# Whole fp32 probability products for four of ten key tiles in two layers' attentions, and a new table of planned durations

## The chip, the cores and the metric

One Trainium2 chip; the kernel runs on one of its cores. The metric is the device time of one execution in microseconds (us). Three executions of the kernel before took 4149.66, 4151.16 and 4156.11 us; their median, 4151.16 us, is the time before.

## The reference, cut to what matters

Everything is float32. The program is two blocks, one after the other. The first block has two layers. Each layer has, over 1024 tokens and 256 context tokens, two kinds of attention with six heads each ("MLA": keys of 96 numbers a head; "GQA": keys of 64 numbers, two key heads for six query heads), a depthwise convolution with 31 taps, gates and an output projection. The attention is plain softmax attention over 1280 keys for the tokens, and (in the first layer only) over the 256 context keys for the context:

```python
s = jnp.einsum('bqgrd,bkgd->bgrqk', qi, k).astype(jnp.float32) * scale
p = jax.nn.softmax(s, axis=-1).astype(v.dtype)
return jnp.einsum('bgrqk,bkgv->bqgrv', p, v)
```

The second block (a gated linear attention, an index selection of the 256 best keys, a sparse attention, a feed-forward net and norms) isn't touched by the change in its arithmetic.

## The kernel before, in words

**Precision.** The program gives TensorE its operands as `float32r` or as `float32`. Where they are `float32r`, a number is split first into a high and a low half, each a `float32r` tile: `N.split` makes the high half with a copy that rounds (line 293 on VectorE or line 284 on ScalarE) and the low half with a subtraction (line 325 on VectorE or line 327 on GpSimd). A product of two split operands is three matmuls: high by high, high by low, low by high.

**The attention.** `attend` (in `layer`, in `block1`) writes one unit of work: one head and one chunk of 512 queries (chunks 0 and 1), or of the 256 context queries (chunk 2, first layer only). A unit first finds the row maximum of the scores (line 368's reductions, and transposes), and then loops over key tiles of 128 keys: ten for chunks 0 and 1, two (tiles 8 and 9) for chunk 2. In each key tile it multiplies keys and queries into PSUM (three passes in MLA, two in GQA), takes the exponential on ScalarE into a float32 page `p` of 128 keys by 512 queries, splits `p` into `ph` and `pl`, and adds three products of 512 columns to the accumulator: `vh` by `ph`, `vl` by `ph`, `vh` by `pl`. A column of ones beside the values gives the sum of the probabilities at once. There are 24 units of 512 queries in each layer, and 12 of 256 in the first.

**The values.** `vtiles` makes the value tiles, two key tiles to a page pair (`a` for the high halves, `b` for the low ones), five page pairs a call, by two transposes, two copies and two subtractions for each, and fills in the ones and zeros on GpSimd. A layer calls it five times (three pairs of MLA heads, two GQA key heads).

**What sets the order.** The program lists its operations in the order of the mathematics, with some merged into others by `merge` and `pipeline`: a unit's start is laid beside the loop of the unit before it. Then a planner, `Plan.schedule`, simulates the five engines with a duration for each operation (the functions `c_act`, `c_v`, `c_p`, and those in `copy`, `ts`, `scale`, `mm`, `tr`), and writes each engine's instructions down in the order in which they started in that simulation. Where an operation may go to either of two engines (a copy to ScalarE or VectorE, a subtraction to VectorE or GpSimd), the simulation also picks the engine: the cheaper one, unless its queue makes the other one sooner. On the chip each engine runs its list in order and waits for what isn't ready. The planner works on the whole program at once, and its buffers (89 pages, 8 PSUM banks) are given out in that same simulation.

**Names.** `pg` is a page in SBUF (128 partitions by 512 numbers), `ps` a PSUM bank, `sm` a small tile, `c` a constant. Line 384 issues every matmul, 388 every transpose, 284 every ScalarE operation, 335 VectorE's operations with a scalar (the convolution's taps and `modulation2` among them).

Of the kernel before, what the change touches and what calls it, by code (L numbers as in the profile page):

```python
# [4 lines left out]
F32 = mybir.dt.float32  # L5
F32R = mybir.dt.float32r
# [18 lines left out]
def _mt(w):  # L25
    k, m = w.shape
    return w.reshape(k // 128, 128, m // 128, 128).transpose(2, 1, 0, 3).reshape(m // 128, 128, k)


V1 = dict(norm=0, bmod=8, qn=32, kvn=34, gq=35, gk=36, dwb=37, lnw=39, lnb=41, pwb=43, dw=45)  # L30
NV1 = 45 + 62
# [130 lines left out]


class Op:
    __slots__ = ("alts", "reads", "writes", "emit", "idx", "succ", "npred", "allocs", "table", "bufs", "tag", "pr", "late")


BASIC = ("Copy", "Identity", "Square", "Abs", "Relu")
# [4 lines left out]
class Plan:  # L173
# [37 lines left out]
    def op(self, alts, reads, writes, emit, table=None):  # L211
        o = Op()
        o.alts = alts
        o.reads = [x for x in reads if isinstance(x, View)]
        o.writes = [x for x in writes if isinstance(x, View)]
        o.emit = emit
        o.table = table
        o.tag = self.tag
        o.late = self.late
        self.cur.append(o)  # L220
        return o
# [37 lines left out]
        return out  # L259

    def c_act(self, n, src, extra=0):
        return (n * 0.833 + (52 if isinstance(src, View) and src.psum else 93) + extra) / 1000

    def act(self, out, in_, func, bias=None, scale=1.0, accum=None, alts=None):
        nc = self.nc
# [31 lines left out]
    def copy(self, out, in_, engs="av"):  # L297
        a = {}
        n = out.n
        if "v" in engs:  # L300
            a["v"] = (n * (1.04 if in_.psum else 0.52) + 68) / 1000
        if "a" in engs:
            return self.act(out, in_, "Copy", alts=a)
        return self.op(a, [in_], [out], lambda e: self._copy(e, out, in_))
# [2 lines left out]
        return {"v": self.nc.vector, "p": self.nc.gpsimd}[e]  # L307

    def c_v(self, n, ex=0):
        return (n * 1.04 + 68 + ex) / 1000  # L310

    def c_p(self, n):
        return (n * 2.1 + 150) / 1000

    def tt(self, out, in0, in1, op, engs="v"):
        o = getattr(OP, op)
# [23 lines left out]
    def ts(self, out, in0, s1, s2, op0, op1=None, accum=None):  # L340
        o0 = getattr(OP, op0)
        k = {} if op1 is None else {"op1": getattr(OP, op1)}

        def emit(e):
            if accum is not None:
                k["accum_out"] = real(accum)
            self.nc.vector.tensor_scalar(out=real(out), in0=real(in0), scalar1=real(s1), scalar2=real(s2), op0=o0, **k)  # L347

        return self.op({"v": (out.n * (1.04 if in0.psum or accum is not None else 0.52) + 130 + (127 if accum is not None else 0)) / 1000},
                       [in0, s1, s2], [out, accum], emit)  # L350

    def scale(self, out, in_, col):

        n = out.n

        def emit(e):
            if e == "a":
                self.nc.scalar.activation(real(out), real(in_), AF.Copy, scale=real(col))
            else:
                self.nc.vector.tensor_scalar(out=real(out), in0=real(in_), scalar1=real(col), scalar2=None, op0=OP.mult)  # L360

        return self.op({"v": (n * (1.04 if in_.psum else 0.52) + 130) / 1000, "a": self.c_act(n, in_, 93)},
                       [in_, col], [out], emit)

    def red(self, out, in_, op="max"):
# [13 lines left out]

    def mm(self, out, lhsT, rhs, start, stop, cost=None):  # L380
        n = rhs.n
        c = cost or max(n * 1.676 if rhs.ap.dtype == F32 or n < 256 else n * 0.4219, 60) / 1000
        return self.op({"t": c}, [lhsT, rhs] + ([] if start else [out]), [out],
                       lambda e: self.nc.tensor.matmul(real(out), lhsT=real(lhsT), rhs=real(rhs), start=start, stop=stop))  # L384

    def tr(self, out, in_, ident):
        return self.op({"t": 0.109}, [in_, ident], [out],
                       lambda e: self.nc.tensor.transpose(real(out), real(in_), real(ident)))  # L388

    def dma(self, out, in_, cost=None):  # L390
# [10 lines left out]
    def schedule(self, window=1500, dwindow=1200, boost=0, queue=0.25, verbose=False):  # L401
# [8 lines left out]
        for o in ops:  # L410
            preds = set()
            bufs = {}
# [110 lines left out]
        while len(order) < N:  # L523
            progress = False
            for e in engs:
                while busy[e] <= now + 1e-9:

                    h = ready[e]
                    skipped = []
                    got = None  # L530
                    best_alt = None
                    while h:
                        i, o = heapq.heappop(h)
                        if issued[o.idx]:
                            continue
                        ok = admissible(o, e)
                        if ok and len(o.alts) > 1:

                            m = min(o.alts, key=lambda x: o.alts[x])
                            if m != e:  # L540
                                wait = max(0.0, busy[m] - now) + queue * min(len(ready[m]), 12)
                                if wait + o.alts[m] < o.alts[e]:
                                    ok = False
                        if ok and e == "a" and o.table is not None and o.table != table:
                            if best_alt is None:
                                best_alt = o
                            skipped.append((i, o))
                            if len(skipped) > 24:
                                break
                            continue  # L550
                        if ok:
                            if best_alt is not None and i > best_alt.pr + 60:
                                skipped.append((i, o))
                                break
                            got = o
                            break
                        skipped.append((i, o))
                        if len(skipped) > 200:
                            break
                    if got is None and best_alt is not None:  # L560
                        got = best_alt
                        skipped = [s for s in skipped if s[1] is not got]
                    for s in skipped:
                        heapq.heappush(h, s)
                    if got is None:
                        break
                    o = got
                    issued[o.idx] = True
                    progress = True
                    c = o.alts[e]  # L570
                    pre = None
                    if e == "a" and o.table is not None and o.table != table:
                        pre = o.table
                        table = o.table
                        c += 1.3
                    new = [b for b in o.allocs if b.slot is None]
                    for b in new:
                        if b.cls in free:
                            need[b.cls][head:o.idx] += 1
                            first[b] = head  # L580
                        b.slot = free[b.cls].pop() if b.cls in free else 0
                    if e == "d":
                        st = max(now + 1.5, dmabw[0])
                        dmabw[0] = st + c
                        fin = st + c + 0.6
                        busy[e] = now + 0.45
                        stat[e] += c
                    else:
                        busy[e] = now + c
                        fin = now + c  # L590
                        stat[e] += c
                    order.append((now, e, o, pre, new))
                    seq += 1
                    heapq.heappush(ev, (fin, 0, seq, o, e))
                    heapq.heappush(ev, (busy[e], 1, seq, None, e))
                    while head < N and issued[head]:
                        head += 1
# [174 lines left out]
def block1(N, O, early, dbg=None):  # L772
# [85 lines left out]
    def layer(l, h, xsrc, xdst, after):  # L858
# [209 lines left out]
        def attend(c, passes, qmax, kmax, nrow, negrow, vt, pos, scale, gate, yf, units, main, back=1):  # L1068
# [27 lines left out]
            for kt in kts:  # L1096
# [3 lines left out]
                N.mm(s, [(kk[kc][:, ks], qq) for kk, qq in passes])  # L1100
                p = fpg(c)
                P.act(p, s, "Exp", scale=scale)
                ph, pl = pair(c)
                split(ph, pl, p)
                vh, vl = (x[:, pos * 64:pos * 64 + 128] for x in vt[kt])
# [21 lines left out]
        def vtiles(src, sel):  # L1127

            out = {}
            for i in range(5):  # L1130
                a, b = P.pg(F32R), P.pg(F32R)
                kc, j = (2, 0) if i == 4 else (i // 2, (i % 2) * 256)
                tp = P.ps(256)
                for t in range(2):
                    P.tr(tp[:, t * 128:(t + 1) * 128], src[kc][:, j + t * 128:j + (t + 1) * 128], N.ident)
                tv = tp.rearrange("p (t b e) -> p t b e", t=2, b=2)
                av = a.rearrange("p (t b e) -> p t b e", t=2, b=2)
                bv = b.rearrange("p (t b e) -> p t b e", t=2, b=2)
                for dst, s_ in sel:
                    P.copy(av[:, :, dst, 0:64], tv[:, :, s_, :])  # L1140
                    lo(bv[:, :, dst, 0:64], tv[:, :, s_, :], av[:, :, dst, 0:64])
                P.memset(av[:, :, 0, 64:128].f(), 1.0)
                P.memset(bv[:, :, 0, 64:128].f(), 0.0)
                for t in range(2):
                    out[2 * i + t] = (a[:, t * 256:t * 256 + 192], b[:, t * 256:t * 256 + 192])
# [895 lines left out]
```

## Time and profile before

| what | value |
|---|---|
| median of three runs | 4151.16 us |
| the profiled execution's own time | 4150.0 us |
| its span, first to last instruction | 4148.1 us |
| mean granted TensorE clock | 0.98 of full speed |
| TensorE matmul busy | 94% of the span |
| VectorE busy | 80% |
| ScalarE busy | 49% |
| GpSimd busy | 34% |

In the profile PE is TensorE's matmul, PEld its weight load, DVE VectorE, ACT ScalarE, POOL GpSimd. A matmul's record lasts from its start to the modelled end of its pipeline, so neighbouring records overlap: the busy time of PE is a union of such records, and the distance from one record to the next is what a matmul costs in a dense stream. Each row of a group ends with the group's busy time, the mean duration of one, and the idle time of the engine just before them with the instruction that ended it. In the profile's list of forms a float32r matmul and a float32 one look alike (`f32`).

### The profile page before, as it was taken

To read this page: it belongs to the slowest core of one execution; us is meant where nothing else is said; L and a number is where in the kernel's file an instruction comes from. 1 tells how busy PE (TensorE), PEld (TensorE's weight loads), DVE (VectorE), ACT (ScalarE), POOL (GpSimd) and SP (SyncE) were. 2 spreads that over 40 slices of the span, in tenths; PEclk is the share of its full clock that TensorE was granted. 3 is DMA by queue.
4 is the path that set the end of the run, shared out by engine and by line. 5 is a ranking of instruction groups with operands and counts; after the bars stand their busy time and mean duration, and the time that the engine had idled before them with its cause. 6 is when DMAs were issued, how large, how long until landed. Compare 5 with 4: busy or idle time off the path is not lost. (4 is left out here: it accounts for less than half of the span.)

```text
span 4148.1 us, 54250 instructions
## 1 busy us (share of the span) xinstructions
PE 3908.4 (94%) x18536; PEld 3153.5 (76%) x18536; DVE 3306.3 (80%) x5640; ACT 2036.4 (49%) x3969; POOL 1430.2 (34%) x1257
## 2 busy tenths in 40 slices
PE   7989998989989998999999999999999999999988
PEld 4768766667877776778878878888878788888867
DVE  8995899997896789985999996388886865455588
ACT  5244576774334566763545551366663432222245
POOL 4542455663142344552223441011132411121153
PEclk8999999999999999999999999999999999999998
DMA  7132211123323110042111142100044411111121
GB/s 254 62 117 72 62 54 53 50 70 114 110 83 99 39 34 26 16 133 94 67 44 54 67 142 77 62 31 30 32 144 152 137 51 49 49 41 46 56 82 57
DMA packets 184981, 311.88 MB, mean 75 GB/s; under 512 B 22912, under 2 KB 46208, under 8 KB 184704
## 3 DMA queue, kind: packets, MB, share of 16 engines
q1 hardware_dynamic: 184704, 308.42, 23.0%
q8 instruction: 146, 2.39, 0.2%
q14 instruction: 131, 1.07, 0.1%
HBM read 237.81 MB, written 62.39 MB: 72 GB/s over the span
## 5 line engine op out<-in xcount | busy, mean ns | idle before, releaser
L384 PE MATMUL ps<-pg,pg 128*128 128x512 f32 (+4 forms) x17200 | 3843.6, 380 | 119.1 <-ACT pg L284 43.5
L384 PEld LDWEIGHTS ps<-pg,pg 128*128 128x128 f32 (+2 forms) x17200 | 3009.0, 190 | 798.5 <-ACT pg L284 72.9
L327 POOL TENSOR_TENSOR pg<-pg,pg 128x512 fp32r<-128x512 f32 (+4 forms) x935 | 1355.7, 1462 | 2338.7 <-ACT pg L284 1301.7
L284 ACT ACTIVATE pg<-pg 128x512 fp32r<-128x512 f32 (+9 forms) x1529 | 875.5, 601 | 893.5 <-DVE pg L335 240.6
L325 DVE TENSOR_TENSOR pg<-pg,pg 128x512 fp32r<-128x512 f32 (+8 forms) x1126 | 956.2, 868 | 218.7 <-ACT pg L284 162.6
L284 ACT ACTIVATE pg<-ps 128x512 f32<-128x512 f32 (+9 forms) x1351 | 686.8, 557 | 801.4 <-PE ps L384 597.4
L325 DVE TENSOR_TENSOR pg<-ps,pg 128x128 fp32r<-128x128 f32 (+9 forms) x690 | 381.3, 567 | 209.2 <-PE ps L384 146.3
L335 DVE SCALAR_TENSOR_TENSOR pg<-ux,c,pg 128x512 f32<-128x512 f32 x416 | 348.7, 867 | 9.6 <-ACT pg L284 2.2
L368 DVE TENSOR_REDUCE sm<-ps 128x1 f32<-128x512 f32 (+1 forms) x492 | 326.1, 679 | 9.6 <-PE ps L384 7.0
L293 DVE CAST pg<-pg 128x512 fp32r<-128x512 f32 (+4 forms) x387 | 226.9, 596 | 72.0 <-ACT pg L284 34.0
L284 ACT ACTIVATE pg<-ps,c 128x512 f32<-128x512 f32 (+1 forms) x182 | 127.3, 708 | 250.0 <-PE ps L384 218.5
L335 DVE SCALAR_TENSOR_TENSOR pg<-pg,c,pg 128x512 f32<-128x512 f32 (+3 forms) x242 | 220.1, 946 | 5.5 <-ACT pg L284 5.2
L388 PE MATMUL ps<-c,pg 128*128 128x128 f32 (+1 forms) x796 | 180.2, 274 | 14.3 <-DVE pg L293 5.8
L293 DVE COPY ux<-ps 128x512 f32<-128x512 f32 x83 | 57.3, 690 | 143.3 <-ACT pg L284 133.6
L1523 DVE MAX8 sm<-ux 128x8 f32<-128x384 f32 (+5 forms) x192 | 168.8, 887 | 3.3
L1524 DVE MATCH_REPLACE8 ux<-sm,ux 128x384 f32<-128x384 f32 (+5 forms) x192 | 167.7, 875 | 0.0
L384 PE MATMUL ps<-pg,c 128*128 128x512 f32 (+3 forms) x196 | 85.2, 502 | 74.9 <-DVE pg L325 28.6
L388 PEld LDWEIGHTS ps<-c,pg 128*128 128x128 f32 (+1 forms) x796 | 107.6, 141 | 40.3 <-issue 6.2
L284 ACT ACTIVATE pg<-pg,sm 128x512 f32<-128x512 f32 (+2 forms) x192 | 116.2, 606 | 11.2 <-DVE sm L347 10.7
L384 PEld LDWEIGHTS ps<-pg,c 128*128 128x128 f32 (+2 forms) x196 | 33.6, 176 | 105.7 <-DVE pg L325 31.6
L671 ACT ACT_TABLE_LOAD x84 | 107.8, 1283 | 1.5
L1778 DVE CUSTOM_DVE_ANT_0 pg<-ps,pg 128x512 f32<-128x512 f32 (+3 forms) x176 | 100.0, 575 | 8.5 <-PE ps L384 6.3
(74 smaller groups left out, 1017.2 us busy)
## 6 DMA issues: line engine op xcount, KB each, us to landing
d<-pg SPq DMA_DIRECT2D x202, 256.0 KB, 2.1
pg<-d SPq DMA_DIRECT2D x178, 256.0 KB, 3.3
pg<-in_w2a SPq DMA_DIRECT2D x108, 256.0 KB, 2.8
pg<-in_wmod SPq DMA_DIRECT2D x96, 256.0 KB, 3.1
pg<-in_wup SPq DMA_DIRECT2D x88, 256.0 KB, 2.7
pg<-in_win SPq DMA_DIRECT2D x80, 256.0 KB, 3.3
pg<-in_wout SPq DMA_DIRECT2D x64, 256.0 KB, 3.3
pg<-in_wdn SPq DMA_DIRECT2D x48, 256.0 KB, 2.7
```

The source lines that it names most:

```text
L284: nc.scalar.activation(real(out), real(in_), fn, scale=real(scale), **k)
L293: self.nc.vector.tensor_copy(real(out), real(in_))
L325: self.nc.vector.tensor_tensor(out=real(out), in0=real(in0), in1=real(in1), op=o)
L327: self.nc.gpsimd.tensor_tensor(out=real(out), in0=real(in0), in1=real(in1), op=o)
L335: self.nc.vector.scalar_tensor_tensor(out=real(out), in0=real(in0), scalar=real(scalar), in1=real(in1), op0=o0, op1=o1)
L368: lambda e: self.nc.vector.tensor_reduce(out=real(out), in_=real(in_), axis=AX.X, op=o))
L384: lambda e: self.nc.tensor.matmul(real(out), lhsT=real(lhsT), rhs=real(rhs), start=start, stop=stop))
L388: lambda e: self.nc.tensor.transpose(real(out), real(in_), real(ident)))
L671: nc.scalar.preload_act_table_set(pre)
L1523: P.vec(P.c_v(n), [w], [m8], lambda e, m8=m8, w=w: nc.vector.max(real(m8), real(w)))
L1524: P.vec(P.c_v(n), [w, m8], [w], lambda e, m8=m8, w=w: nc.vector.match_replace(real(w), real(m8), real(w), MARK))
L1778: lambda e, p=p, s=s, n=n, m=mk[t, b], a=sm[:, b:b + 1]: nc.vector.tensor_tensor_reduce(out=real(p), in0=real(s[:, 0:n]), in1=real(m), sca ...
```

## The change

It does three things.

1. Value tiles 2, 3, 6 and 7 (the pages `i` of `WHOLE = (1, 3)` in `vtiles`) are kept as one float32 page instead of a pair of halves; the two subtractions and one memset of each such page go. In `attend`, a key tile whose value is whole takes one float32 matmul of `p` itself, without the split of `p`, in place of the three float32r matmuls. This holds for the units of 512 queries in both layers; the context's units use only tiles 8 and 9, which stay split.
2. The planner's durations are changed for every operation of the program.
3. The planner lengthens a VectorE operation that reads pages only (with over 64 elements a partition) if GpSimd is busy when it starts: by 0.42 of the overlap.

```diff
+WHOLE = (1, 3)
...
+        o.dual = "v" in alts and not any(x.psum for x in o.reads) and sum(x.n > 64 for x in o.reads) > 0
...
     def c_act(self, n, src, extra=0):
-        return (n * 0.833 + (52 if isinstance(src, View) and src.psum else 93) + extra) / 1000
+        return (n * 0.836 + (170 if isinstance(src, View) and src.psum else 202) + extra) / 1000
...
-            a["v"] = (n * (1.04 if in_.psum else 0.52) + 68) / 1000
+            a["v"] = (n * (1.04 if in_.psum else 0.52) + 155) / 1000
...
     def c_v(self, n, ex=0):
-        return (n * 1.04 + 68 + ex) / 1000
+        return (n * 1.04 + 155 + ex) / 1000
 
     def c_p(self, n):
-        return (n * 2.1 + 150) / 1000
+        return (n * 2.2 + 200) / 1000
...
-        c = cost or max(n * 1.676 if rhs.ap.dtype == F32 or n < 256 else n * 0.4219, 60) / 1000
+        c = cost or max(n * 1.774 if rhs.ap.dtype == F32 or n < 256 else n * 0.4434 + 1, 60) / 1000
...
-        return self.op({"t": 0.109}, [in_, ident], [out],
+        return self.op({"t": 0.06}, [in_, ident], [out],
...
                     c = o.alts[e]
+                    if e == "v" and o.dual and busy["p"] > now:
+                        c += 0.42 * min(busy["p"] - now, c / 0.58)
...
                 p = fpg(c)
                 P.act(p, s, "Exp", scale=scale)
+                if len(vt[kt]) == 1:
+
+                    P.mm(acc, vt[kt][0][:, pos * 64:pos * 64 + 128], p, kt == kts[0], kt == kts[-1])
+                    continue
                 ph, pl = pair(c)
...
-                a, b = P.pg(F32R), P.pg(F32R)
+                whole = i in WHOLE
+                a = P.pg() if whole else P.pg(F32R)
...
+                for dst, s_ in sel:
+                    P.copy(av[:, :, dst, 0:64], tv[:, :, s_, :])
+                P.memset(av[:, :, 0, 64:128].f(), 1.0)
+                if whole:
+                    for t in range(2):
+                        out[2 * i + t] = (a[:, t * 256:t * 256 + 192],)
+                    continue
+                b = P.pg(F32R)
```

The constants in `ts` and `scale` change in the same way (130 to 190 ns for VectorE).

## Rows read from the trace of the kernel before

**Rows 1.** The page's head and its first part, busy time by engine.

```profile
span 4148.1 us, 54250 instructions
PE 3908.4 (94%) x18536; PEld 3153.5 (76%) x18536; DVE 3306.3 (80%) x5640; ACT 2036.4 (49%) x3969; POOL 1430.2 (34%) x1257
```

**Rows 2.** Reductions of line 368 by stretch: stretch, length, DVE busy (count), PEclk, DMA.

```profile
430.00:990.00 560.00, 169.88 (x274) 0.97 0.20 61
1360.00:1840.00 480.00, 161.73 (x264) 0.98 0.13 40
```

**Rows 3.** All engines by stretch: stretch, length, PE PEld DVE ACT POOL, PEclk, DMA.

```profile
430.00:990.00 560.00, 505.69 (x2268) 382.93 (x2267) 531.16 (x809) 387.02 (x746) 330.35 (x282) 0.97 0.20 61
1360.00:1840.00 480.00, 445.67 (x1907) 335.12 (x1906) 434.76 (x670) 321.64 (x588) 245.72 (x230) 0.98 0.13 40
3400.00:3500.00 100.00, 99.90 (x440) 82.16 (x439) 49.50 (x69) 24.80 (x40) 11.70 (x13) 1.00 0.16 50
```

**Rows 4.** Groups by shape, 3400 to 3500 us, TensorE.

```profile
L384 PE MATMUL ps<-pg,pg 128*128 128x512 f32 x440 | 100.3, 390 | 0.1
```

**Rows 5.** Groups by shape, 430 to 990 us, TensorE.

```profile
L384 PE MATMUL ps<-pg,pg 128*128 128x512 f32 x1085 | 382.4, 426 | 25.9 <-POOL pg L327 5.9 <-DVE pg L325 5.6 <-ACT pg L284 5.3
L384 PE MATMUL ps<-pg,pg 96*128 96x512 f32 x333 | 121.6, 407 | 0.3
L384 PE MATMUL ps<-pg,pg 128*128 128x256 f32 x256 | 72.5, 300 | 2.6 <-ACT pg L284 0.9 <-DVE pg L325 0.8 <-DVE sm L368 0.7
...
L384 PE MATMUL ps<-pg,pg 96*128 96x256 f32 x82 | 24.1, 314 | 8.4 <-DVE sm L368 4.0 <-ACT pg L284 2.4 <-DVE pg L293 2.0
```

**Rows 6.** The same, 1360 to 1840 us, TensorE.

```profile
L384 PE MATMUL ps<-pg,pg 128*128 128x512 f32 x1087 | 352.1, 413 | 15.7 <-DVE pg L293 5.5 <-DVE pg L325 5.5 <-DVE sm L368 2.0
L384 PE MATMUL ps<-pg,pg 96*128 96x512 f32 x336 | 125.5, 410 | 3.4 <-DVE sm L368 3.2
```

**Rows 7.** Timeline of TensorE at 2803 us: start, length, what, how many.

```profile
2802.91 0.49 PE L388 MATMUL ps<-c,pg 128*128 128x128 f32 x3
```

**Rows 8.** Timeline of TensorE at 1889 us, a float32 product of 512 columns.

```profile
1889.85 1.02 PE L384 MATMUL ps<-pg,c 128*128 128x512 f32 x2
```

**Rows 9.** Groups by shape, 430 to 990 us, copies and subtractions.

```profile
L327 POOL TENSOR_TENSOR pg<-pg,pg 128x512 fp32r<-128x512 f32 x191 | 283.1, 1494 | 170.5 <-DVE pg L293 70.7 <-ACT pg L284 65.2 <-PE ps L384 22.3
...
L284 ACT ACTIVATE pg<-ps 128x512 f32<-128x512 f32 x242 | 139.8, 595 | 75.0 <-PE ps L384 69.8 <-DVE pg L325 1.7 <-POOL pg L327 1.6
...
L284 ACT ACTIVATE pg<-pg 128x512 fp32r<-128x512 f32 x197 | 120.6, 629 | 21.3 <-DVE pg L325 9.7 <-DVE pg L335 8.1 <-ACT pg L284 0.4
L325 DVE TENSOR_TENSOR pg<-pg,pg 128x512 fp32r<-128x512 f32 x87 | 84.7, 979 | 4.1 <-ACT pg L284 3.2
L335 DVE SCALAR_TENSOR_TENSOR pg<-pg,c,pg 128x512 f32<-128x512 f32 x84 | 82.4, 993 | 0.2
...
L293 DVE CAST pg<-pg 128x512 fp32r<-128x512 f32 x81 | 54.4, 678 | 5.5 <-ACT pg L284 4.3 <-PE ps L384 0.3
...
L325 DVE TENSOR_TENSOR pg<-ps,pg 128x128 fp32r<-128x128 f32 x40 | 11.2, 282 | 1.2 <-issue 0.9
```

**Rows 10.** The same, 1360 to 1840 us.

```profile
L327 POOL TENSOR_TENSOR pg<-pg,pg 128x512 fp32r<-128x512 f32 x153 | 216.1, 1422 | 204.4 <-DVE pg L293 83.0 <-ACT pg L284 82.6 <-PE ps L384 23.4
...
L284 ACT ACTIVATE pg<-pg 128x512 fp32r<-128x512 f32 x177 | 108.9, 630 | 10.7 <-DVE pg L325 5.6 <-PE ps L384 0.8
L325 DVE TENSOR_TENSOR pg<-pg,pg 128x512 fp32r<-128x512 f32 x107 | 105.6, 993 | 3.7 <-PE ps L384 1.4 <-ACT pg L284 0.4
...
L293 DVE CAST pg<-pg 128x512 fp32r<-128x512 f32 x86 | 58.0, 681 | 9.1 <-ACT pg L284 8.1 <-PE ps L384 0.3
```

**Rows 11.** Timeline of VectorE at 802 us, operations that GpSimd did not hold up.

```profile
802.18 0.42 DVE L293 CAST pg<-pg 128x512 fp32r<-128x512 f32 x1
...
804.58 0.69 DVE L325 TENSOR_TENSOR pg<-pg,pg 64x512 f32<-64x512 f32 x1
```

**Rows 12.** Groups by shape, 100 to 330 us, GpSimd beside the convolution.

```profile
L327 POOL TENSOR_TENSOR pg<-pg,pg 128x512 fp32r<-128x512 f32 x40 | 89.8, 2255 | 102.4 <-ACT pg L284 61.8 <-DVE pg L293 35.0 <-issue 5.4
```

More of the change, by code (lines that the diff above doesn't have):

```diff
@@ L164 @@
 class Op:
-    __slots__ = ("alts", "reads", "writes", "emit", "idx", "succ", "npred", "allocs", "table", "bufs", "tag", "pr", "late")
+    __slots__ = ("dual", "alts", "reads", "writes", "emit", "idx", "succ", "npred", "allocs", "table", "bufs", "tag", "pr", "late")
 BASIC = ("Copy", "Identity", "Square", "Abs", "Relu")
@@ L347, in emit @@
             self.nc.vector.tensor_scalar(out=real(out), in0=real(in0), scalar1=real(s1), scalar2=real(s2), op0=o0, **k)
-        return self.op({"v": (out.n * (1.04 if in0.psum or accum is not None else 0.52) + 130 + (127 if accum is not None else 0)) / 1000},
+        return self.op({"v": (out.n * (1.04 if in0.psum or accum is not None else 0.52) + 190 + (127 if accum is not None else 0)) / 1000},
                        [in0, s1, s2], [out, accum], emit)
@@ L360, in emit @@
                 self.nc.vector.tensor_scalar(out=real(out), in0=real(in_), scalar1=real(col), scalar2=None, op0=OP.mult)
-        return self.op({"v": (n * (1.04 if in_.psum else 0.52) + 130) / 1000, "a": self.c_act(n, in_, 93)},
+        return self.op({"v": (n * (1.04 if in_.psum else 0.52) + 190) / 1000, "a": self.c_act(n, in_, 93)},
                        [in_, col], [out], emit)
@@ L1137, in vtiles @@
                 av = a.rearrange("p (t b e) -> p t b e", t=2, b=2)
+                for dst, s_ in sel:
[6 more added lines that the diff above has]
+                b = P.pg(F32R)
                 bv = b.rearrange("p (t b e) -> p t b e", t=2, b=2)
                 for dst, s_ in sel:
-                    P.copy(av[:, :, dst, 0:64], tv[:, :, s_, :])
                     lo(bv[:, :, dst, 0:64], tv[:, :, s_, :], av[:, :, dst, 0:64])
-                P.memset(av[:, :, 0, 64:128].f(), 1.0)
                 P.memset(bv[:, :, 0, 64:128].f(), 0.0)
```

## The prediction

> **What bounds the kernel now.** I read the page's head first, then the split of the span into stretches, and then the shapes inside the stretches that the change touches. The head says that matmuls cover 94% of the span and VectorE 80% [rows 1]; by that alone one would say that TensorE is full, and that a change which gives it more columns loses. The stretches say otherwise. The attentions are where line 368's reductions lie: 274 of them from 430 to 990 us (first layer) and 264 from 1360 to 1840 us (second layer) [rows 2]. There matmul records cover 506 of 560 and 446 of 480 us, while VectorE is busy 531 of 560 (95%) and 435 of 480 (91%) [rows 3].
>
> The cover overstates TensorE, because a record holds the tail of its pipeline. In the feed-forward stretch, where TensorE hardly waits, 440 matmuls of 512 columns take 99.9 us [rows 3, 4], so one costs 0.227 us, though its record is 0.390 long [rows 4]; the tail is 0.163. Counted at this step, the first layer's stretch holds 1085 + 333 [rows 5] and 240 more (six GQA heads, and six MLA heads' first pass, by two chunks by ten key tiles), so 1658 matmuls of 512 columns, 376 us. The matmuls of 256 columns, 256 + 82 in two rows and 24 more, are 362 at half a step, 41 us. There are 160 transposes (96 + 24 of the maxima, 40 of the value tiles, by the code) at 0.109 us: three in 0.49 less the tail of 0.163 [rows 7]; 17 us. That is 435 us of matmul in 560, 78%. The second layer has 1087 + 336 + 240 = 1663 [rows 6], 377 us, 96 of 256 columns by the code, 11, and 136 transposes, 15: 403 of 480, 84%. So TensorE has 125 and 77 us to spare here, in small gaps that end on GpSimd, VectorE and ScalarE alike [rows 5, 6], and VectorE is the engine that is full.
>
> In a sentence beside this: the Trainium skill, Perfetto Trace Analysis, Identifying the Most-Contended Engine, warns that the busy share of matmuls is a poor measure and points to the share of the weight loads; that share is 383 of 560 (68%) in the first attention against 82% in the feed-forward stretch [rows 3], so by that rule TensorE would stand at 83% of what it does when full, and the trace agrees with my 78% in direction.
>
> **The change part by part.**
>
> *The added matmul.* A float32 product of 512 columns is in the trace as two records: 1.02 us with the tail [rows 8], so 0.857. It takes the place of three steps, 0.681. Each whole key tile costs 0.176 us more on TensorE. There are 24 units of four such tiles in a layer, 96 tiles: +17 us a layer, 34 us in all, if nothing hides it. TensorE then has 452 us to do in the first stretch and 420 in the second.
>
> *The split that goes.* 96 copies and 96 subtractions of 128 by 512 go in each layer. I take them off the engines in the shares that these have now. First layer: subtractions 191 on GpSimd, 87 on VectorE; copies 197 on ScalarE, 81 on VectorE [rows 9]. So 66 subtractions leave GpSimd (x 1.494 = 99 us), 30 leave VectorE (x 0.979 = 29), 68 copies leave ScalarE (x 0.629 = 43) and 28 leave VectorE (x 0.678 = 19). Second layer, 153 to 107 and 177 to 86 [rows 10]: GpSimd loses 56 x 1.422 = 80, VectorE 40 x 0.993 + 31 x 0.681 = 61, ScalarE 65 x 0.630 = 41 us.
>
> *The value tiles.* Two of five pages in five calls lose two subtractions of 0.282 us each [rows 9]: 20 a layer, 5.6 us of VectorE. Ten memsets go from GpSimd, which isn't full; I cost them at nothing. The copies stay.
>
> *What VectorE's other operations gain.* A copy takes 0.42 and a subtraction 0.69 us where GpSimd doesn't hold it up [rows 11], but 0.678 and 0.979 on average here [rows 9]. The surcharge is 81 x 0.26 + 87 x 0.29 = 46 us. About seven tenths of these operations stay, and three tenths of GpSimd's time (99 of 330 us) goes: 10 us. Second layer the same way (86 x 0.26 + 107 x 0.30 = 54, x 0.65, x 80/246): 11 us. In sentences of their own: the Trainium skill, SBUF, Two separate sides, has the port that the two share as an exclusive lock held for a whole instruction. Were every microsecond of GpSimd one that VectorE stands still, the 99 us would come back whole; the surcharge of 46 us against 283 us of subtractions on GpSimd [rows 9] says that only a sixth does.
>
> *The sum.* VectorE in the first stretch: 531 - 29 - 19 - 6 - 10 = 467 us. If it stays the bound, at the same share, the stretch becomes 560 x 467 / 531 = 492 us. TensorE's 452 us would at 92% of use take 491: both ask for about 492, and the gain is 68 us. In the second stretch VectorE falls to 435 - 61 - 6 - 11 = 357, which alone would give 394; TensorE's 420 us don't fit there, at 92% they take 457. The gain is 23 us. The 92% is chosen between the 78 and 84% of now and the full use of the feed-forward stretch, since the order there still has chains of maxima and exponentials. Its ends: at 97% the stretches become 466 and 433 us, a gain of 141; at the shares of now (78 and 84%) they become 579 and 500, a loss of 39.
>
> *Waits and queues.* The whole product waits for the exponential on ScalarE (0.595 us [rows 9]) where the split ones waited for copy and subtraction too, so behind it on TensorE's queue nothing is held longer than now. `p` stays one page until its matmul ends, where three were held. The DMA share is 0.20 and 0.13 here [rows 3]; nothing is moved past the SP queue that waits on it. If scores no longer come from a late VectorE, the next thing late is ScalarE's exponential (242 in 560 us, ScalarE busy 387 [rows 3, 9]) or the reductions of line 368.
>
> *The planned durations.* They add no work; they change the order and the engine of every operation. Against the rows: ScalarE from a page 0.520 becomes 0.630 (row 0.629), from PSUM 0.479 becomes 0.598 (row 0.595); VectorE's subtraction 0.600 becomes 0.687, or up to 1.18 beside GpSimd (row 0.979); GpSimd's 1.225 becomes 1.326 (row 1.494) [rows 9]. A matmul of 512 columns 0.216 becomes 0.228 (0.227). Two go off: a transpose 0.109 becomes 0.060 (0.109 [rows 7]), and a float32 product 0.858 becomes 0.908 (0.857 [rows 8]). On the whole the plan comes closer, above all for VectorE in the attentions, and I count that as what lifts TensorE's use from 78 to 92% there. Outside the two stretches I take nothing. The bounds there: matmul records leave 152 us uncovered (4148 - 3908 [rows 1], less 54 and 34 in the stretches [rows 3]), and a third of it might close, -50; on the other side, beside the convolution a subtraction on GpSimd takes 2.255 us [rows 12], 0.93 more than planned, and 40 of them sent there and found on TensorE's path would cost 37.
>
> Together: 4150 (the profiled execution) - 68 - 23 = 4059 us. The median of the runs is 1 us above that execution, so 4060.
>
> **The rivals.**
>
> *TensorE was full all along (slower).* If the stretch is held by chains (maximum, exponential, product) and not by VectorE's load, TensorE keeps its 78 and 84%, and the added columns come on top: +34 to +39, some 4187 us. For it: the head's 94%, and cover of 90% and 93% in the stretches [rows 1, 3]. Against it: VectorE's 95%, idle time of TensorE in many small pieces with three engines as releasers [rows 5], and GpSimd's waits, which end on VectorE's and ScalarE's copies [rows 9]. It decides if the gaps that close are under 34 us in all. 10%.
>
> *Only part of the relief arrives.* The planner sees VectorE free and puts back on it what ScalarE and GpSimd did; TensorE ends near 85% in the first stretch and 88% in the second: 452 / 0.85 = 532 and 420 / 0.88 = 477, a gain of 31, some 4120. For it: the choice of an engine follows queues, which shorten everywhere. Against: GpSimd's and ScalarE's shares (59 and 69%) leave room. 18%.
>
> *More than that.* TensorE at 97% in the stretches (-141) or 92% there and the other stages' gaps closed by a third (-141 too): some 4010. For it: a plan nearer to the rows. Against: two durations moved away from them, and the chains of maxima and exponentials stay. 12%.
>
> *The change doesn't do what it says,* so that nothing moves by over 0.2% (8 us; less can't be told from no change here): gains and losses would have to meet by chance. 5%.
>
> **How the numbers follow.** The forecast case, 55%, runs from 4020 to 4105 us. Faster by over 0.2%: 55 + 18 + 12 = 85%. Same: 5%. Slower: 10%. The range is 4000 to 4145: below it lies about half of the third rival, above it the slower one and most of the case of no change, some 20% together.
>
> **What would show it.** In the trace after, TensorE's records in the attentions should show 192 float32 products (two records each), the copies and subtractions of 128 by 512 should be fewer by 96 each in a layer, VectorE's share in the first attention should fall under 95% or the stretch be nearer to 490 than to 560 us, and the second to 457; VectorE's mean subtraction should come under 0.979 us. If the stretches stay as long and the records cover more, the first rival holds. If the gain lies outside the attentions, my account of the planned durations is wrong.

## The result, and the profile after

The changed kernel takes 3983.79 us (median of four runs, 3982.97 to 3984.50) against 4150.41: ratio 0.9597, 95% interval 0.958 to 0.9614. That is 167 us faster where 91 were forecast, below the range.

The page of the kernel after begins like this, to be held against [rows 1]:

```profile
span 3982.5 us, 53245 instructions
PE 3860.4 (97%) x18344; PEld 3100.5 (78%) x18344; DVE 3130.6 (79%) x5241; ACT 1964.9 (49%) x3841; POOL 1520.0 (38%) x1348
```

TensorE issues 192 matmuls fewer, as it should (192 tiles, two records for three). GpSimd is busier than before, though 192 subtractions are gone: the plan sent it others.

The reductions of line 368 are line 373 now. The same 274 and 264 of them lie in these stretches (columns as in [rows 2], then as in [rows 3]):

```profile
410.00:905.00 495.00, 170.80 (x274) 1.00 0.23 71
1260.00:1701.00 441.00, 161.37 (x264) 1.00 0.15 45
...
410.00:905.00 495.00, 485.67 (x2190) 361.24 (x2189) 454.80 (x714) 342.69 (x665) 270.02 (x248) 1.00 0.23 71
1260.00:1701.00 441.00, 436.24 (x1807) 315.48 (x1806) 368.42 (x586) 277.10 (x506) 192.86 (x188) 1.00 0.15 45
```

The first attention went from 560 to 495 us, the second from 480 to 441. The reader is to see TensorE's cover rise to 98 and 99%, VectorE's share fall from 95 to 92 and from 91 to 84%, and the granted clock rise from 0.97 and 0.98 to 1.00. The groups behind it, first stretch and then second (to be held against [rows 5, 6, 9, 10]):

```profile
L389 PE MATMUL ps<-pg,pg 128*128 128x512 f32 x995 | 358.4, 455 | 6.2 <-POOL pg L332 1.8 <-DVE pg L330 1.6 <-DVE pg L298 1.4
...
L332 POOL TENSOR_TENSOR pg<-pg,pg 128x512 fp32r<-128x512 f32 x143 | 204.4, 1437 | 167.9 <-DVE pg L298 73.9 <-ACT pg L289 59.2 <-PE ps L389 14.9
...
L289 ACT ACTIVATE pg<-pg 128x512 fp32r<-128x512 f32 x109 | 67.1, 627 | 15.3 <-DVE pg L330 5.0 <-DVE pg L340 4.2 <-POOL pg L332 2.6
L298 DVE CAST pg<-pg 128x512 fp32r<-128x512 f32 x75 | 52.0, 699 | 6.5 <-ACT pg L289 5.6
...
L330 DVE TENSOR_TENSOR pg<-pg,pg 128x512 fp32r<-128x512 f32 x41 | 39.5, 965 | 2.8 <-issue 0.7 <-PE ps L389 0.7 <-ACT pg L289 0.7
...
L389 PE MATMUL ps<-pg,pg 128*128 128x512 f32 x987 | 342.4, 453 | 2.4 <-DVE pg L298 1.1 <-ACT pg L289 0.9 <-POOL pg L332 0.3
...
L332 POOL TENSOR_TENSOR pg<-pg,pg 128x512 fp32r<-128x512 f32 x119 | 162.4, 1375 | 205.4 <-DVE pg L298 113.4 <-ACT pg L289 55.1 <-issue 15.9
...
L330 DVE TENSOR_TENSOR pg<-pg,pg 128x512 fp32r<-128x512 f32 x50 | 42.8, 861 | 9.3 <-ACT pg L289 4.4 <-PE ps L389 3.7
```

In the first stretch subtractions fell from 278 to 184 and copies from 278 to 184. TensorE's idle time before its main group fell from 25.9 to 6.2 us, and in the second stretch from 15.7 to 2.4.

Where the 167 us lie is best seen by stages, with edges that every kernel has: the first and last reduction of each attention, the first and last of the sparse attention's maxima. Lengths in us, from the traces:

| stage | before | after | whole products alone | plan alone | engines before, order new | engines new, order before |
|---|---|---|---|---|---|---|
| to the first attention | 428 | 408 | 426 | 404 | 397 | 440 |
| first attention | 527 | 462 | 497 | 519 | 549 | 525 |
| between | 410 | 395 | 404 | 397 | 392 | 413 |
| second attention | 457 | 418 | 435 | 432 | 431 | 451 |
| to the sparse attention | 846 | 817 | 853 | 817 | 820 | 845 |
| sparse attention | 418 | 429 | 419 | 429 | 429 | 420 |
| rest | 1061 | 1053 | 1062 | 1052 | 1046 | 1061 |

The attentions gave 65 + 38 = 103 us and the rest 63, its one loss being the sparse attention's 10. The last four columns are kernels of the experiments; each column is one profiled execution.

### The profile page after: what moved, and what is told of

It is laid out like the page before. It is cut to its first block, busy times and chain, and to the rows that moved or that the text cites. A ratio compares the mean times of both kernels' runs of the same rounds, so it can differ in the third digit from the quotient of the medians.

```text
span 3982.5 us, 53245 instructions
## 1 busy us (share of the span) xinstructions
PE 3860.4 (97%) x18344; PEld 3100.5 (78%) x18344; DVE 3130.6 (79%) x5241; ACT 1964.9 (49%) x3841; POOL 1520.0 (38%) x1348
## 5 line engine op out<-in xcount | busy, mean ns | idle before, releaser
L389 PE MATMUL ps<-pg,pg 128*128 128x512 f32 (+5 forms) x17008 | 3789.5, 384 | 43.6 <-ACT pg L289 19.8
L389 PEld LDWEIGHTS ps<-pg,pg 128*128 128x128 f32 (+3 forms) x17008 | 2955.4, 188 | 733.5 <-issue 72.9
L332 POOL TENSOR_TENSOR pg<-pg,pg 128x512 fp32r<-128x512 f32 (+4 forms) x1030 | 1437.2, 1411 | 2015.2 <-ACT pg L289 1037.8
L289 ACT ACTIVATE pg<-pg 128x512 fp32r<-128x512 f32 (+7 forms) x1385 | 785.7, 596 | 779.4 <-DVE pg L340 252.1
L289 ACT ACTIVATE pg<-ps 128x512 f32<-128x512 f32 (+10 forms) x1352 | 681.8, 551 | 870.3 <-PE ps L389 708.2
L330 DVE TENSOR_TENSOR pg<-pg,pg 128x512 fp32r<-128x512 f32 (+7 forms) x839 | 769.5, 930 | 150.9 <-ACT pg L289 99.2
L330 DVE TENSOR_TENSOR pg<-ps,pg 128x512 fp32r<-128x512 f32 (+9 forms) x650 | 367.5, 584 | 223.3 <-PE ps L389 133.9
L298 DVE CAST pg<-pg 128x512 fp32r<-128x512 f32 (+4 forms) x342 | 210.9, 623 | 56.2 <-ACT pg L289 24.9
L393 PE MATMUL ps<-c,pg 128*128 128x128 f32 (+1 forms) x796 | 163.8, 272 | 11.4 <-DVE pg L298 6.0
L383 POOL MEMSET pg<- 128x128 f32 (+2 forms) x193 | 49.9, 274 | 159.7 <-PE ps L389 99.0
```

Source lines behind the costliest of these rows:

```text
L289: nc.scalar.activation(real(out), real(in_), fn, scale=real(scale), **k)
L298: self.nc.vector.tensor_copy(real(out), real(in_))
L330: self.nc.vector.tensor_tensor(out=real(out), in0=real(in0), in1=real(in1), op=o)
L332: self.nc.gpsimd.tensor_tensor(out=real(out), in0=real(in0), in1=real(in1), op=o)
```

## The experiments

Medians of four runs and more, ratio to the kernel before on the same chip with its 95% interval.

**The two halves of the change.** The whole products with all planned durations put back (`e1_arith`), and the new durations with all tiles split (`e2_plan`: `WHOLE = ()`).

> The whole products alone: four of ten key tiles in float32, with the planner's durations of before. Theory L (load: the attentions gain because VectorE, ScalarE and GpSimd lose work; the new durations gain only outside the attentions): the attentions give all of the 103 us that lie between their first and last reductions in the two traces, about 4047 us. Theory P (plan: TensorE's gaps come from an order written for too short durations, so the freed work alone closes only part of them): the attentions give 40 to 60 us, about 4090 to 4110 us.

> The new durations and the rule for a busy GpSimd alone; all ten key tiles split as before. Theory L: only the 63 us outside the attentions, about 4087 us, and the attentions' stretches stay at 527 and 457 us between first and last reduction. Theory P: the attentions get shorter too, by 40 us or more together, so 4045 us or less.

Measured: 4096.25 us (0.9864, 0.9848 to 0.988) and 4051.94 us (0.9758, 0.9743 to 0.9773). So 54 us come with the arithmetic and 99 with the plan, 153 together; the 13 left come from having both. Theory L falls: the arithmetic gives only 52 of the attentions' 103 us, and the plan shortens them by 33, not by nothing (theory P had 40 or more, and 4045 us or less: a near miss). By the traces the arithmetic alone gives 1 us outside the attentions, the plan alone 65. In the first attention of the arithmetic alone VectorE's operations are shorter, as GpSimd is less in their way; copies and subtractions of the kernel with whole products alone, 428 to 957 us:

```profile
L330 DVE TENSOR_TENSOR pg<-pg,pg 128x512 fp32r<-128x512 f32 x67 | 56.8, 850 | 10.3 <-ACT pg L289 8.7 <-PE ps L389 0.5
...
L298 DVE CAST pg<-pg 128x512 fp32r<-128x512 f32 x62 | 36.0, 582 | 15.8 <-ACT pg L289 14.0 <-PE ps L389 1.0
```

A subtraction went from 0.979 to 0.850 us and a copy from 0.678 to 0.582 [rows 9]. That this goes with GpSimd can be read from single operations. Between the first and the last reduction of the first attention of the kernel before, 18 of 72 such subtractions have no GpSimd instruction beside them and take 0.68 us on average; the other 54 take 1.13. With whole products alone, 25 of 55 have none beside them.

**Constants or rule.** All tiles split, with the constants alone (`e3_const`, whose edit is shown) and with the rule for a busy GpSimd alone on the constants of before (`e4_dual`).

```diff
-                    if e == "v" and o.dual and busy["p"] > now:
+                    if False and e == "v" and o.dual and busy["p"] > now:
```

> The new constants without the rule for a busy GpSimd, all tiles split. If the constants do the work (ScalarE +0.11, VectorE +0.09, GpSimd +0.10 us for 512 elements), the time is within 15 us of the run with constants and rule. If the rule does it (only it knows that VectorE takes 0.98 and not 0.69 us beside GpSimd), the time is within 25 us of before, 4125 us or more.

> The rule for a busy GpSimd alone, on the constants of before, all tiles split. If the rule does the work: within 20 us of the run with constants and rule. If the constants do it: within 25 us of before. If both are needed alike, each of the two runs has about half of the gain.

Measured: 4126.66 us (0.9939, 0.9924 to 0.9953) and 4073.19 (0.9811, 0.9796 to 0.9825): -24 and -77 of the 99. The rule is the larger part, and the two add up.

**Engines or order.** By then I took it that the plan gains by moving subtractions from VectorE to GpSimd (935 on GpSimd before, 1167 with the new plan). These two plan twice: the first pass only picks each operation's engine, the second writes the order with the other set of durations.

```diff
+    DUR[0] = PICK
+    P = listed(tc, I, O, dbg, verbose)
+    P.schedule(verbose=verbose, **OPTS)
+    picked = {o.sn: e for t, e, o, pre, new in P.order}
+    DUR[0] = 1 - PICK
+    P = listed(tc, I, O, dbg, verbose)
+    for o in P.cur:
+        o.alts = {picked[o.sn]: o.alts[picked[o.sn]]}
```

> All tiles split. The engine of every operation is the one that the plan with the new durations and rule picked; the order is then planned with the durations of before. Theory E (engines: the plan gains because it sends 232 more subtractions from VectorE to GpSimd): near the run of the new plan, 4052 us, at most 25 us above it. Theory O (order: truer durations make each engine's list fit what the others deliver): within 25 us of before, 4125 us or more.

> All tiles split. The engine of every operation is the one of the kernel before; the order is planned with the new durations and rule. Theory E: within 25 us of before, 4125 us or more. Theory O: near the run of the new plan, at most 25 us above 4052 us. If both count, each of the two kernels has a good part of the 99 us.

Measured: new engines in the order of before 4159.83 us (1.002, 1.001 to 1.0029); engines of before in the new order 4062.39 (0.9787, 0.9773 to 0.9802). Theory E falls, and with it what I believed of the plan. Moving 232 subtractions gives nothing without the order; the order gives 89 of 99 us without the move. But the total hides that the stages differ (the table's last two columns). Outside the attentions the order alone gives 81 us, more than the whole plan's 65, and the move alone loses 14. In the first attention the order alone loses 22 us, and the stage is 549 us long; with the move on top, which is the plan alone, it is 519, so there the move is worth 30 us once the order is new. Between first and last reduction of that attention (columns as in [rows 3]), in the kernel before, with the engines of before in the new order, and with the plan alone:

```profile
428.00:956.00 528.00, 476.21 (x2123) 359.53 (x2122) 504.38 (x776) 366.82 (x709) 316.10 (x273) 0.97 0.20 58
```

```profile
397.00:946.00 549.00, 498.21 (x2142) 373.27 (x2140) 506.78 (x770) 358.98 (x705) 317.27 (x281) 0.94 0.19 57
```

```profile
404.00:923.00 519.00, 482.59 (x2150) 362.79 (x2149) 491.48 (x712) 382.40 (x746) 354.19 (x305) 0.98 0.20 60
```

GpSimd's subtractions in the pages of the two kernels show that the picks were as meant for the new engines (1167), and nearly so for those of before (946 against 935):

```profile
L336 POOL TENSOR_TENSOR pg<-pg,pg 128x512 fp32r<-128x512 f32 (+4 forms) x1167 | 1643.4, 1426 | 2008.7 <-ACT pg L293 977.8
```

```profile
L336 POOL TENSOR_TENSOR pg<-pg,pg 128x512 fp32r<-128x512 f32 (+5 forms) x946 | 1352.5, 1444 | 2218.9 <-ACT pg L293 1087.5
```

What the order does is plainest beside the convolution. The same 300 us from 100 to 400 (columns as in [rows 3]), in the kernel before,

```profile
100.00:400.00 300.00, 270.18 (x1350) 223.78 (x1350) 262.82 (x386) 119.60 (x213) 127.86 (x81) 0.96 0.25 81
```

with the engines of before in the new order,

```profile
100.00:400.00 300.00, 293.31 (x1518) 245.37 (x1518) 277.33 (x427) 130.61 (x240) 128.43 (x100) 0.99 0.29 94
```

and with the new engines in the order of before:

```profile
100.00:400.00 300.00, 265.81 (x1297) 221.15 (x1298) 249.52 (x340) 116.22 (x208) 149.35 (x96) 0.93 0.26 84
```

In the new order TensorE issues 168 matmuls more and VectorE is busy 14.5 us longer in the same time. The granted clock goes with it, 0.96 to 0.99. TensorE's waits in that stretch (who waited for whom, us in all, times, longest) are, in the kernel before,

```profile
PE ps L384 <- DVE pg L293: 10.6, 4, 4.7
PE ps L384 <- POOL pg L327: 9.1, 7, 5.9
PE ps L384 <- ACT pg L284: 6.7, 2, 5.3
PE ps L384 <- DVE pg L325: 4.4, 3, 2.5
```

with the engines of before in the new order,

```profile
PE ps L393 <- ACT pg L293: 2.7, 4, 0.9
PE ps L393 <- DVE pg L302: 2.3, 1, 2.3
PE ps L393 <- DVE pg L334: 1.0, 2, 0.6
PE ps L393 <- POOL pg L336: 0.3, 2, 0.2
```

and with the new engines in the order of before:

```profile
PE ps L393 <- DVE pg L302: 17.3, 5, 8.0
PE ps L393 <- ACT pg L293: 13.7, 7, 3.4
```

The reader is to see 31 us of waits become 6, the long ones gone from this stretch, with nearly the same engine for every operation; and 31 us and more stay where only the engines are new.

**Truer, or only other?** Any change of durations reshuffles the lists. Two drawings of random factors between 0.98 and 1.02 on the durations of before:

```diff
+        f = 1 + 0.02 * self.rng.uniform(-1, 1)
+        o.alts = {e: t * f for e, t in alts.items()}
```

> The kernel before, with each operation's planned duration multiplied by a random number between 0.98 and 1.02 (first drawing). Theory T (truth: an order written for truer durations fits the chip better): the lists are reshuffled without being truer, so the time stays within 10 us of 4150. Theory R (reshuffling: this kernel's order is one drawing among many, and any change of durations draws again): the time moves by 20 us or more in either direction.

> The same with a second drawing of the random numbers. Theory T: within 10 us of 4150. Theory R: 20 us or more off, and not where the first drawing landed. The spread of the two is the size below which a difference between two orders says nothing of the durations.

Measured: 4155.72 us (1.0012, 1.0002 to 1.0022) and 4145.79 (0.9984, 0.9974 to 0.9993): 4 and 5 us off. Reshuffling by 2% is worth 5 us, not 99. The change itself is far larger: VectorE's subtraction was planned 15% longer, and up to 97% with the rule. No random drawing of that size was run, nor a large change away from the trace, so that the truth of the new durations makes the gain, and not their size, is argued and not shown. For it speaks that the two prices of VectorE lie near what the trace of before shows: 0.687 us against 0.68 with no GpSimd instruction beside, and up to 1.18 against 1.13 with one.

**Whose durations.** All tiles split; VectorE's constants and the rule alone:

> All tiles split; the rule for a busy GpSimd and VectorE's constants new, the constants of ScalarE, GpSimd and TensorE as before. If the gain of the new plan is knowing how long VectorE takes: 4052 us, at most 15 above it. If ScalarE's and TensorE's constants have a share of their own: 4070 us or more, near the run with the rule alone (4073).

Measured: 4054.67 us (0.9768, 0.9753 to 0.9782), 3 us from the whole plan. The other engines' constants count for nothing that can be told from a reshuffle. Then only `scalar_tensor_tensor` (the taps) with the new price and rule, and all of VectorE's but that:

```diff
+        r = self.op({"v": self.c_v(out.n, 60 + 87 * ONLY)}, [in0, scalar, in1], [out], emit)
+        r.dual = not any(x.psum for x in r.reads) and sum(x.n > 64 for x in r.reads) > 0
```

> All tiles split; new VectorE duration (87 ns more, and the rule for a busy GpSimd) for scalar_tensor_tensor alone, that is for the convolution's taps, modulation2 and a few others; all other durations as before. Theory F (filler: the short price let the plan lay taps into VectorE's seeming gaps, ahead of what TensorE waits for): the stages before and between the attentions give their 35 us and the gated linear attention some, 4105 us or less. Theory A (all of VectorE's durations count alike): the stages with taps give under 15 us, 4130 us or more.

> All tiles split; VectorE's new durations and the rule for all its operations but scalar_tensor_tensor. Theory F: the stages before and between the attentions stay as before (428 and 410 us), the attentions gain, about 4095 us. Theory A: most of the 96 us, 4075 us or less.

Measured: 4107.27 us (0.99, 0.9885 to 0.9914) and 4068.66 (0.9801, 0.9785 to 0.9817). Neither theory holds as put. The taps' price gives 13 us ahead of the first attention (428 to 416), where the other operations' price gives 1; between the attentions and towards the sparse one it is the reverse (3 and 0 against 12 and 27 us), and 17 of the taps' 41 us lie in the first attention, where `modulation2` runs. Both prices together give 24 us ahead of the first attention. Which price a stage answers to isn't simply a matter of which operations crowd it: the taps take as much of VectorE beside the second layer's convolution, between the attentions (956 to 1366 us), as beside the first (100 to 400 us), in the trace of before,

```profile
L335 DVE SCALAR_TENSOR_TENSOR pg<-ux,c,pg 128x512 f32<-128x512 f32 x120 | 98.8, 870 | 0.1
```

```profile
L335 DVE SCALAR_TENSOR_TENSOR pg<-ux,c,pg 128x512 f32<-128x512 f32 x120 | 99.5, 881 | 0.5
```

(the first convolution, then the second), and their price gave 13 us in the one stage and 3 in the other. Why stays open.

**Whether TensorE is the bound now.** Eight of ten tiles whole:

```diff
-WHOLE = (1, 3)
+WHOLE = (0, 1, 2, 3)
```

> The changed kernel with eight of ten key tiles whole. If TensorE is now the bound in the attentions, 192 further tiles at 0.176 us come on top, 34 us, less what gaps are left: 4005 to 4020 us. If VectorE still binds (busy 91% and more between first and last reduction), the split that goes gives back as much: 3984 us or less.

Measured: 3989.87 us (0.9612, 0.9598 to 0.9626), below the range of the one theory and above the other. The attentions became 5 and 10 us longer, with another 192 copies and subtractions gone; between first and last reduction (columns as in [rows 3]):

```profile
403.00:871.00 468.00, 464.93 (x1956) 324.06 (x1955) 392.66 (x652) 286.56 (x556) 135.44 (x148) 1.00 0.23 68
1264.00:1692.00 428.00, 425.60 (x1633) 285.58 (x1631) 312.48 (x530) 236.01 (x420) 53.71 (x78) 1.00 0.14 43
```

TensorE is covered 99%, VectorE busy 84 and 73%: relief no longer pays. Cover overstates, so count by the step: between first and last reduction lie 1403 and 1396 matmul records of 512 columns, 384 of each for the 192 float32 products (0.857 us a product), 312 and 106 of 256 columns and 158 and 132 transposes. That is 448 of 468 us and 421 of 428, or 96 and 98%. Of the 34 us of columns 15 show in the attentions. The other stages together are 9 us shorter, and the whole is 6 us slower, with an interval that overlaps that of the changed kernel.

**The two durations that went off the rows.** Transpose and float32 product put back to what the trace shows, both (`e7_tr109`) and the transpose alone (`e14_tr`):

```diff
-        return self.op({"t": 0.06}, [in_, ident], [out],
+        return self.op({"t": 0.109}, [in_, ident], [out],
```

> The changed kernel with two planned durations put back to what the trace shows: a transpose 0.109 instead of 0.060 us, a float32 matmul 1.676 instead of 1.774 ns a column. If the short transpose is what made the sparse attention 10 us longer (418 to 429 us), that stage comes back to about 418 and the whole to about 3974 us. If that is the other constants, the stage stays at 425 or more and the whole within 5 us of 3984.

> The changed kernel with the planned transpose alone put back to 0.109 us (the float32 matmul stays at 1.774 ns a column). If the 14 us that both cost came with the transpose: about 3998 us. If with the float32 product's price: about 3984 us. If it was one drawing among several of about 5 us each: in between.

Measured: 3997.94 us (0.9627, 0.9611 to 0.9643) and 3991.09 (0.9619, 0.9605 to 0.9634). Truer prices here didn't make it faster: the medians are 14 and 7 us higher, though both intervals overlap that of the changed kernel (0.958 to 0.9614), the first just. The sparse attention came back by 3 of its 10 us. A step of 5 to 15 us between two orders says nothing of the durations' truth.

**A version beside.** GpSimd's durations raised by 8% (`e12_pool`), and the same with ScalarE's constants of before (`e13_act`):

```diff
-        return (n * 2.2 + 200) / 1000
+        return (n * 2.2 + 200) * 1.08 / 1000
```

> The changed kernel with GpSimd's planned durations raised by 8%, to 1.43 us for a subtraction of 512, where its trace shows 1.41 on average over all shapes. Theory T: truer again, so 3984 us or less, by up to 15 us. Theory R: anywhere within 15 us of 3984, above it as likely as below.

> The changed kernel with GpSimd's durations raised by 8% and ScalarE's constants of before. If ScalarE's constants are what made the sparse attention 10 us longer: that stage comes back to 418 to 420 us and the whole to about 3970 us. If not, the stage stays at 425 us or more and the whole is 3978 us or more.

Measured: 3977.60 us (0.9582, 0.9568 to 0.9596) and 3991.89 (0.962, 0.9606 to 0.9635). The first is the lowest time of all, but its interval overlaps that of the changed kernel, so it isn't shown to be faster. The sparse attention stays at 427 us in both, so ScalarE's constants aren't what lengthened it. It is 417 with the rule alone, 424 with VectorE's durations and 426 with the constants alone; the cause stays open.

## Why the prediction was wrong

**The step that failed** is "Outside the two stretches I take nothing". It measured -63 us, and the bound of -50 set beside it was too narrow. The bound was a third of the time that matmul records leave uncovered (152 us), the very measure that the first part had set aside because a record holds its tail. From 100 to 400 us the cover leaves 30 us of 300. The groups by shape of the kernel before in that stretch begin with

```profile
L384 PE MATMUL ps<-pg,pg 128*128 128x512 f32 x818 | 246.0, 404 | 1.5 <-DVE pg L325 1.5
L384 PE MATMUL ps<-pg,pg 128*128 128x256 f32 x428 | 116.7, 286 | 2.2 <-ACT pg L284 1.4 <-DVE pg L325 0.3 <-POOL pg L327 0.2
```

and hold 48 and 24 more of these widths in smaller groups. At 0.227 and half of it that is 866 x 0.227 + 452 x 0.114 = 248 us, so 52 us were to spare, not 30. The step was read at a granted clock of 1.00 and the mean clock here is 0.96, so by an estimate 12 of the 52 us are the clock's (0.04 x 300). Counted so over all stages outside the attentions, with transposes at 0.109 us, the trace of before leaves some 270 us, not 152; the changed kernel is 63 us shorter there, about a quarter of it.

**The reason behind it** was a wrong picture of what a planned duration does. Outside the attentions I priced only the work that the durations would move between engines, where GpSimd was slow (2.255 us [rows 12]), and not the order. The plan alone gives 65 us outside, the arithmetic 1; the pair of kernels with engines and order exchanged shows that the order alone gives 81 there and the move alone loses 14. VectorE's durations alone suffice for the whole of the plan's gain (4055 us). One row that told this stood in the text, for the first attention: VectorE's subtraction was planned at 0.600 us and took 0.979. In the trace of before it took 0.81 to 0.90 us in the stages ahead of, between and behind the attentions too (the sparse attention, which has four, left out).

**What bounds, in the attentions:** right. TensorE had 125 and 77 us to spare; taking splits away, with the plan of before, gave 30 and 22 us there, and with eight whole tiles TensorE's steps fill 96 and 98% and the stages get longer.

**The added matmul:** two records for three, as forecast; its 0.176 us could not be seen by themselves: 192 more of them lengthened the attentions by 15 us and not by 34.

**The split that goes:** 94 fewer copies and subtractions in the first stretch against 96. The shares differ: VectorE lost 46 of its 87 subtractions, not 30, and GpSimd 48, not 66, as the new plan sends more of them to GpSimd.

**VectorE's other operations:** 10 and 11 us were put. With whole products alone, the first attention shows 67 x 0.129 + 62 x 0.096 = 15 us. In the changed kernel the term is nearly gone there: a subtraction takes 0.965 us against 0.979 and a copy 0.699 against 0.678, as GpSimd keeps more work (270 us of the stretch, where 330 less 99 would be 231). In the second stretch a subtraction takes 0.861 against 0.993 us and a copy 0.683 against 0.681, so 50 x 0.132 = 7 us.

**The sum of the attentions:** 492 forecast and 495 measured; 457 forecast and 441 measured, where TensorE's 420 us make 95% of use instead of 92. Together 104 against 91 us. That the first lies so near is in part luck: VectorE, which was put at 467 us and 95% of the stretch, had 455 and stood at 92%, by other terms than those put. And the reason given, that the plan lifts TensorE's use, holds for half: arithmetic alone gave 52, plan alone 33, and 18 came only with both.

**The rivals:** TensorE was not full all along. "More than that" named the other stages' gaps as one of its two ways, at 12%; it was this way, and further than its 4010 us.

## What to carry to other kernels

Where a planner writes each engine's list, its durations are part of the kernel: price the crowded engine as the trace shows it, contention included, and don't only move work off it. When such a price changes, count spare time in every stage by the step of a matmul, not by the cover of its records, and look beyond the stage that the change is about. Two random drawings of the durations tell how large a difference between orders must be to mean anything (here 5 us, with later variants 14 us apart).

## What the runs showed of the hardware

The mean granted clock rose from 0.980 to 0.990, so by an estimate the clock withheld fell from 83 to 40 us of the span (0.020 x 4148 and 0.010 x 3982). In the attentions the granted clock went from 0.97 and 0.98 to 1.00, beside the convolution from 0.96 to 0.99, each time where TensorE's waits went. Some of the gain may thus be matmuls at full speed. How much wasn't separated from the waits themselves, so it isn't shown, and the prediction had no term for it.

VectorE's subtraction of 128 by 512 took 0.68 us on average with no GpSimd instruction beside it and 1.13 with one (first attention, kernel before); a copy took 0.42 and 0.87.
